# First activation tile on ScalarE's DMA queue, and FFN1's first pair of groups with P7 ahead of P5, in a float32 macaron block on one Trainium2 core

## Chip, core and metric

The kernel runs on one core of a Trainium2 chip. The metric is the device time of one execution in microseconds (us); the median of three timed executions of the kernel before is 2192.64 us (2191.59 to 2192.67).

TensorE (PE) does the matrix products and loads its weights beside them (PEld). VectorE (DVE) and ScalarE (ACT) prepare operands and take results out of the accumulator banks. SyncE (SP) issues transfers. GpSimd (POOL) does nothing here after its first microsecond.

## What is computed

A block over 1024 tokens of 1024 features, all in float32, cut to what matters:

```python
h = x + 0.5 * swiglu(rmsnorm(x), ffn1_w_in, ffn1_w_out)      # FFN1: D_FF = 2816
u = rmsnorm(h)
q, k, v, g_ret, p, gates = split(u @ w_in)
ret  = retention(rotary(q), rotary(k), v)  ...  * silu(g_ret)
pool = multiscale_pool(p)
h = h + (sigmoid(g0) * (ret @ w_ret_up) + sigmoid(g1) * (pool @ w_pool_up)) @ w_out
h = h + 0.5 * swiglu(rmsnorm(h), ffn2_w_in, ffn2_w_out)      # FFN2
out = rmsnorm(h)

def swiglu(x, w_in, w_out):
    gate, up = split(x @ w_in, 2)
    return (silu(gate) * up) @ w_out
```

The change touches only the first microseconds and the first three groups of FFN1's first product, `rmsnorm(x) @ ffn1_w_in`.

## The kernel before

**Layout.** Activations lie transposed: a tile has 128 features on the partitions and 1024 tokens along the row; `half(t, j)` is tokens 512j to 512j+511. `x` is eight such tiles, `x[0]` to `x[7]`, loaded in half tiles of 256 KB ("quarters"). A weight tile `raw` is 128 x 1024.

**Exact float32 products.** Every operand is split into a high and a low part: ScalarE rounds it into the high part (`split` line 146, or `split_scaled` line 150, which also multiplies by the norm's gain out of the tile `vec`), and VectorE subtracts (line 147 or 151) for the low part. `mm3` (lines 166 to 168) then issues three matmuls: high x high, high x low, low x high. Every matmul is preceded by a weight load. The names in the trace follow: `n1R` and `n1T` are FFN1's activation operands, `a_wL` and `a_wS` weight operands, digits left out.

**Strassen in seven products.** `strassen` (line 353) computes a 256-wide group of outputs, a gate tile and an up tile, from 2 x 2 blocks. The weight blocks are L11, L12 (the two halves of `ra`) and L21, L22 (of `rb`), with S1 = L21 + L22, S2 = S1 - L11, S3 = L11 - L21, S4 = L12 - S2. The activation blocks are R11, R12 (tiles 0 to 3, the two token halves) and R21, R22 (tiles 4 to 7), with T1 = R12 - R11, T2 = R22 - T1, T3 = R22 - R12, T4 = R21 - T2. The products use three accumulator banks:

- P1 = L11 R11 into bank a, which ScalarE copies into bank b (line 397)
- P2 = L12 R21 onto a; a is the result (0, 0), taken out by ScalarE (line 530)
- P6 = S2 T2 onto b; b is copied to v (line 402)
- P5 = S1 T1 onto b
- P7 = S3 T3 into bank e, copied to p7 by ScalarE (line 419)
- when both P5 and P7 are done, result (1, 1) = b + p7, by VectorE (`fourth` line 404, `evac` line 525). It reads b, so P3 of the same group can't write b before it is done
- P3 = S4 R22 onto b: result (0, 1), taken out by ScalarE (line 530)
- P4 = L22 T4 onto e: result (1, 0) = e + v, by VectorE (line 525)

A product has 4 x 3 = 12 matmuls of 128 x 128 by 128 x 512.

**The order of products.** `strassen` returns its steps at positions 0 to 6 in the order P1, P6, P5, P7, P2, P3, P4, each a pair (prepare the weights, do the product). `BY_OPERAND` = (0, 4, 1, 3, 2, 6, 5) is therefore P1, P2, P6, P7, P5, P4, P3. FFN1's groups come in the order 0, 11, 1, 12, 2, ... Group 0 is done without Strassen (`plain_group` line 579: 8 steps of 12 matmuls on R11, R21, R12, R22), so that TensorE can start while T1 to T4 are made. Groups 11 and 1 are the first pair: `in_turn` (line 449) takes each position for the one, then for the other. All later groups of FFN1 are done one at a time in the order P1, P7, P6, P2, P5, P4, P3.

**Program order.** `Flow.run` (line 64) issues the weight preparation of a step four steps ahead of its product, and after each product takes one piece of other work from a list (`flow.back`); a product that needs an operand takes pieces until it is there (`flow.until`). The list for FFN1 is filled at line 814: R11, R21, R12, gain on R22, R22, T2, T1, T3, T4, four pieces each (one for each pair of tiles), then eight pieces `x_square` (line 817: load a tile of x by tokens, square it on ScalarE and sum along the row), then `roots` (the norm's inverse roots, which use ScalarE's square root, line 201) and `rows` (spread over the partitions through TensorE, lines 219 and 335). The compiler's scheduler then arranges each engine's own sequence, with that order as its priority; on the chip each engine works through its sequence in order.

**Buffers that matter here.** Half tiles `c2`: 8, for the differences t1 (made with T2, read by T1), S1 to S4, v and p7. Weight operands `wt`: 5. Activation tiles `t4`: 9, of which x takes 8. Tiles `tl`: 4, of which group 0's results hold two and `x_square` uses the others.

**Loads at the start.** All transfers go through `load` (line 133), which is SyncE's queue: `vec` (line 176), then, from line 805, the weight block L11 of group 0, x[0] to x[3] tokens 0 to 511, L21, L12, x[4] to x[7], L22, then the second token half of x.

Of the kernel before, what the change touches and what calls it, by code (L numbers as in the profile page):

```python
# [20 lines left out]
KT = D // P  # L21
H = S // 2  # L22
# [30 lines left out]
BY_OPERAND = (0, 4, 1, 3, 2, 6, 5)  # L53
# [36 lines left out]
def block_kernel(ctx: ExitStack, tc, x, x_tok, vecs, f1_in, f1_out, w_in, pool_w, w_ret, w_pool, w_o,  # L90
                 f2_in, f2_out, rope, decay, consts, out):
    nc = tc.nc
# [21 lines left out]
    def raw(name):  # L114
        return sb.tile([P, S], F32, tag="raw", bufs=N_RAW, name=name)
# [4 lines left out]
    def t4(name):  # L120
        return sb.tile([P, S], F32, tag="t4", bufs=N_T4, name=name)

    def c2(name):
        return sb.tile([P, H], F32, tag="c2", bufs=N_C2, name=name)
# [8 lines left out]
    def load(dst, src):  # L133
        nc.sync.dma_start(dst, src)
# [4 lines left out]
    def half(t, j):  # L139
        return t[:, j * H : (j + 1) * H]  # L140
# [32 lines left out]
    vec = cp.tile([P, NV], F32, name="vec")  # L173
    neg = cp.tile([P, NV], F32, name="neg")
    cst = cp.tile([P, NC], F32, name="cst")
    load(vec, vecs)

    warm = cp.tile([P, 1], F32, name="warm")
# [68 lines left out]
    class Next(Norm):  # L247
# [22 lines left out]
        def g(self, mt, v=None):  # L270
            if self.gain is None:
                return None
            v = vec if v is None else v
            return v[:, self.gain + mt : self.gain + mt + 1]
# [174 lines left out]
    def in_turn(groups, order=range(7), first=2):  # L449

        groups = list(groups)
        steps = [g() for g in groups[:first]]
        for n in order:
            for g in steps:
                yield g[n]

        for g in groups[first:]:
            steps = g()
            for n in (0, 3, 1, 4, 2, 6, 5):
                yield steps[n]  # L460
# [49 lines left out]
    def ffn_in(nx, w, ops, name, start=None):  # L510

        R, T, B, T4 = ops
        hid = {}

        def group(g):
            gate_up = []

            def evac(which, in0, in1):
                if not gate_up:
                    new = tl if start and g == 0 else t4  # L520
                    gate_up.extend((new(f"{name}g{g}"), new(f"{name}u{g}")))
                tile, j = which
                dst = half(gate_up[tile], j)
                if in1 is not None:
                    tt(dst, in0, in1, ADD)
                elif nx.rb is not None:
                    tt(dst, in0, half(nx.rb, j), MUL)
                    return
                else:
                    copy(dst, in0)  # L530
                flow.add(lambda: tt(dst, dst, half(nx.rms(), j), MUL))

            def end():
                gate, up = gate_up

                def swish():
                    act(gate, gate, AF.Silu)

                def times(j):
                    tt(half(up, j), half(gate, j), half(up, j), MUL)  # L540

                flow.add(swish, lambda: times(0), lambda: times(1))
                hid[g] = up
                k = g % FH
                if g < FH:
                    return
                lo, hi, e = hid.pop(k), up, {}
                R11, R12, R21, R22 = half(lo, 0), half(lo, 1), half(hi, 0), half(hi, 1)

                def w1():  # L550
                    e["n"], e["m"] = t4(f"{name}n{k}"), c2(f"{name}m{k}")
                    tt(half(e["n"], 0), R12, R11, SUB)
                    tt(half(e["n"], 1), R22, R12, SUB)
                    load(B[k], e["n"])

                def w2():
                    tt(R12, R22, half(e["n"], 0), SUB)
                    load(R[k], lo)
                    load(T[k], hi)

                def w3():
                    tt(e["m"], R21, R12, SUB)
                    load(T4[k], e["m"])
                    done.add(k)

                flow.add(w1, w2, w3)

            if start and g == 0:
                return plain_group(nx, start, f"{name}{g}_", evac, end)
            return lambda: strassen(nx, w[g, 0], w[g, 1], f"{name}{g}_", evac, end)  # L570

        done = ops_done.setdefault(name, set())
        order = [g for k in range(FH) for g in (k, k + FH)]
        if start:
            return chain(group(0), in_turn((group(g) for g in order[1:]), (0, 4, 1, 2, 3, 5, 6)))
        return in_turn((group(g) for g in order), BY_OPERAND)


    def plain_group(nx, blocks, name, evac, end):

        t, w = {}, {}

        def step(o, i, j):


            def prep():
                if j == 0:
                    w[o, i] = weights(blocks[2 * o + i], f"{name}w{o}{i}")

            def body():  # L590
                if i == 0:
                    t[o] = bank(f"{name}{o}{j}")
                for k in range(4):
                    mm3(t[o], parts(w[o, i], k), parts(nx.operand(("R11", "R12", "R21", "R22")[2 * i + j], k)),
                        i == 0 and k == 0, i == 1 and k == 3)
                if i == 1:
                    evac((o, j), t[o], None)
                    if (o, j) == (1, 1):
                        end()

            return prep, body

        return [step(o, i, j) for j in range(2) for i in range(2) for o in range(2)]
# [189 lines left out]


    first = Next("n1", V_FFN1)
    xt = {mt: t4(f"x{mt}") for mt in range(KT)}
    ra, rb = raw("ra"), raw("rb")
    lead = half(ra, 0), half(ra, 1), half(rb, 0), half(rb, 1)

    def quarters(j, mts):  # L800
        for mt in mts:
            first.tiles[mt, j] = half(xt[mt], j)
            load(first.tiles[mt, j], x[mt, :, j * H : (j + 1) * H])

    load(lead[0], f1_in[0, 0, :, :H])
    quarters(0, range(4))
    load(lead[2], f1_in[0, 1, :, :H])
    load(lead[1], f1_in[0, 0, :, H:])
    quarters(0, range(4, 8))
    load(lead[3], f1_in[0, 1, :, H:])  # L810
    quarters(1, range(4))
    quarters(1, range(4, 8))
    load(cst, consts)
    first.work(first.r11, first.r21, first.r12, first.r22, first.p22, first.t2, first.t1, first.t3, first.t4_)
    x_sums = sb.tile([P, 8], F32, tag="ss", bufs=2, name="x_sums")

    def x_square(t):
# [14 lines left out]
    def ffn1():  # L832
        for n, step in enumerate(ffn_in(first, f1_in, ops1, "a", lead)):
            flow.rate = 1 if n < 40 else 2
            yield step
        yield from ffn_out(ops1, ops_done["a"], f1_out, x, "b", mix.quarter, end1)
# [133 lines left out]
    order = light[:2] + [o for two in zip(heavy, light[2:14]) for o in two] + light[14:]  # L970
# [401 lines left out]
    def second():  # L1372
        for n, step in enumerate(ffn_in(ffn2, f2_in, ops2, "c")):
            flow.rate = 1 if n < 14 else 2
            yield step
# [84 lines left out]
```

## Time and profile before

| | |
|---|---|
| timed, median of 3 | 2192.64 us (2191.59 to 2192.67) |
| the profiled execution's own time | 2192.35 us |
| its span, first to last instruction | 2190.6 us |
| TensorE's mean granted clock | 0.997 |
| first matmul on real data | 6.15 us |
| group 0 (96 matmuls) ends, P1 of group 11 begins | about 28.6 us |

The trace is of one execution. Times are microseconds from the first instruction. A row of the timeline gives start, duration, engine, line, operation, what it writes and reads, its size, how many were merged, and in brackets how long the engine was idle before it and what ended that. Matmuls are pipelined, so a matmul row's duration is longer than the distance to the next; distances between starts are used below for TensorE's pace.

### The profile page before, as it was taken

What the parts mean: (1) busy time and instruction counts of PE and PEld (TensorE: products, weight loads), DVE (VectorE), ACT (ScalarE), POOL (GpSimd) and SP (SyncE); (2) the same over time, 40 slices, a digit from 0 to 9 for tenths busy, and PEclk for the clock granted to TensorE, in tenths of its full rate; (3) what the DMA queues carried; (4) which work ended last, traced back from release to release, by engine and by line L of the source; (5) the groups of instructions that cost most, each with busy time, mean ns of one, the idle gap of its engine ahead of it and who ended that gap; (6) DMA issues with size and microseconds to landing.
All of it is one profiled execution on the core that took longest, in us unless ns stands there. A gap on an engine that the chain in (4) does not pass through costs nothing.

```text
span 2190.6 us, 27454 instructions
## 1 busy us (share of the span) xinstructions
PE 2171.6 (99%) x10070; PEld 1809.5 (83%) x10070; DVE 1677.5 (77%) x2766; ACT 985.3 (45%) x1756; POOL 0.2 (0%) x4
## 2 busy tenths in 40 slices
PE   9999999999999999999999999999999999999998
PEld 7788888888888888888888998878888888888887
DVE  8687777887786767677776777799977777689775
ACT  8433333444553433434336664446533333344451
POOL 0000000000000000000000000000000000000000
PEclk9999999999999999999999999999999999999999
DMA  6144222495323333323235557524242323249522
GB/s 239 58 154 168 92 104 96 162 334 178 125 92 112 139 116 116 115 105 127 96 124 187 188 180 278 192 87 147 75 144 101 135 92 123 94 158 337 173 73 78
DMA packets 111015, 311.86 MB, mean 142 GB/s; under 512 B 12448, under 2 KB 14624, under 8 KB 110880
## 3 DMA queue, kind: packets, MB, share of 16 engines
q1 hardware_dynamic: 110880, 310.11, 40.0%
q8 instruction: 79, 1.29, 0.2%
q14 instruction: 56, 0.46, 0.1%
HBM read 219.36 MB, written 90.70 MB: 142 GB/s over the span
## 4 chain that ended last, share of the span: by engine, by line
PE 94%; DVE 3%; ACT 2%; DMA 1%; issue 0%; SPq 0%; DVEq 0%; ACTq 0%
PE c_b L166 3%; PE c_b L168 3%; PE c_b L167 3%; PE a_b L168 2%; PE a_b L166 2%; PE a_b L167 2%; PE c_e L166 2%; PE c_a L167 2%; PE c_a L166 2%; PE c_a L168 2%; PE c_e L168 2%; PE c_e L167 2%; PE a_e L168 2%; PE a_e L167 2%; PE a_a L168 2%; PE a_e L166 2%
## 5 line engine op out<-in xcount | busy, mean ns | idle before, releaser
L146 ACT CAST c_wS<-c_S 128x512 fp32r<-128x512 f32 x88 | 54.7, 622 | 124.7 <-PE c_b L168 76.1
L146 ACT CAST a_wS<-a_S 128x512 fp32r<-128x512 f32 x84 | 52.2, 622 | 105.7 <-PE a_b L168 71.0
L147 DVE TENSOR_TENSOR c_wS<-c_S,c_wS 128x512 fp32r<-128x512 f32 x88 | 60.9, 692 | 22.6 <-ACT c_wS L146 22.0
L147 DVE TENSOR_TENSOR a_wS<-a_S,a_wS 128x512 fp32r<-128x512 f32 x84 | 58.2, 693 | 24.4 <-ACT a_wS L146 24.0
L167 PE MATMUL c_a<-n3R,c_wL 128*128 128x512 f32 x176 | 68.6, 390 | 0.0
L167 PE MATMUL c_b<-n3T,c_wS 128*128 128x512 f32 x176 | 68.5, 389 | 0.0
L168 PE MATMUL c_b<-n3T,c_wS 128*128 128x512 f32 x176 | 68.5, 389 | 0.0
L168 PE MATMUL c_a<-n3R,c_wL 128*128 128x512 f32 x176 | 68.5, 389 | 0.0
L166 PE MATMUL c_a<-n3R,c_wL 128*128 128x512 f32 x176 | 68.3, 389 | 0.0
L166 PE MATMUL c_b<-n3T,c_wS 128*128 128x512 f32 x176 | 68.2, 389 | 0.0
L168 PE MATMUL a_a<-n1R,a_wL 128*128 128x512 f32 x168 | 65.4, 389 | 0.0
L166 PE MATMUL a_a<-n1R,a_wL 128*128 128x512 f32 x168 | 65.4, 389 | 0.0
L167 PE MATMUL a_a<-n1R,a_wL 128*128 128x512 f32 x168 | 65.4, 389 | 0.0
L166 PE MATMUL a_b<-n1T,a_wS 128*128 128x512 f32 x168 | 65.4, 389 | 0.0
L167 PE MATMUL a_b<-n1T,a_wS 128*128 128x512 f32 x168 | 65.4, 389 | 0.0
L168 PE MATMUL a_b<-n1T,a_wS 128*128 128x512 f32 x168 | 65.4, 389 | 0.0
L146 ACT CAST c_wL<-c_ra 128x512 fp32r<-128x512 f32 x44 | 27.2, 620 | 38.0 <-PE c_e L168 38.0
L146 ACT CAST a_wL<-a_ra 128x512 fp32r<-128x512 f32 x42 | 26.0, 621 | 37.6 <-PE a_e L168 37.6
L167 PEld LDWEIGHTS c_a<-n3R,c_wL 128*128 128x128 f32 x176 | 33.0, 188 | 7.2 <-DVE n3R L151 0.3
L167 PEld LDWEIGHTS c_b<-n3T,c_wS 128*128 128x128 f32 x176 | 33.0, 188 | 7.0 <-DVE n3T L151 0.2
L147 DVE TENSOR_TENSOR c_wL<-c_ra,c_wL 128x512 fp32r<-128x512 f32 x44 | 30.4, 692 | 10.8 <-ACT c_wL L146 10.5
L168 PEld LDWEIGHTS c_a<-n3R,c_wL 128*128 128x128 f32 x176 | 33.0, 188 | 6.9
(2500 smaller groups left out, 7300.3 us busy)
## 6 DMA issues: line engine op xcount, KB each, us to landing
c_ra<-in_f_in SPq DMA_DIRECT2D x22, 512.0 KB, 3.7
c_rb<-in_f_in SPq DMA_DIRECT2D x22, 512.0 KB, 4.7
a_ra<-in_f_in SPq DMA_DIRECT2D x21, 512.0 KB, 4.5
a_rb<-in_f_in SPq DMA_DIRECT2D x21, 512.0 KB, 5.1
t<-au SPq DMA_DIRECT2D x11, 512.0 KB, 2.6
b<-an SPq DMA_DIRECT2D x11, 512.0 KB, 3.2
r<-au SPq DMA_DIRECT2D x11, 512.0 KB, 3.8
br<-r SPq DMA_DIRECT2D x11, 512.0 KB, 5.4
```

The costliest lines, as they stand in the source:

```text
L146: copy(hi, src)
L147: tt(lo, src, hi.bitcast(F32), SUB)
L166: mm(dst, w[0], m[0], start=start, stop=False, skip_group_check=True)
L167: mm(dst, w[0], m[1], start=False, stop=False, skip_group_check=True)
L168: mm(dst, w[1], m[0], start=False, stop=stop, skip_group_check=True)
```

## The change

Two things are edited. `x[0]`'s first token half is loaded by a transfer that ScalarE issues, at the top of the program, before `vec`; right behind it SyncE issues the load of L11 of group 0, and only then `vec`. (For this the tiles `xt`, `ra` and `rb` are allocated earlier.) And the first pair of groups uses `BY_OPERAND`: P1, P2, P6, P7, P5, P4, P3 in place of P1, P2, P6, P5, P7, P3, P4; in the list of other work T3 comes before T1.

```diff
@@ block_kernel, before the loads
+    xt = {mt: t4(f"x{mt}") for mt in range(KT)}
+    ra, rb = raw("ra"), raw("rb")
+    nc.scalar.dma_start(half(xt[0], 0), x[0, :, :H])
+    load(half(ra, 0), f1_in[0, 0, :, :H])
     load(vec, vecs)
@@ ffn_in
         if start:
-            return chain(group(0), in_turn((group(g) for g in order[1:]), (0, 4, 1, 2, 3, 5, 6)))
+            return chain(group(0), in_turn((group(g) for g in order[1:]), BY_OPERAND))
@@ the loads of FFN1
     first = Next("n1", V_FFN1)
-    xt = {mt: t4(f"x{mt}") for mt in range(KT)}
-    ra, rb = raw("ra"), raw("rb")
     lead = half(ra, 0), half(ra, 1), half(rb, 0), half(rb, 1)
 
     def quarters(j, mts):
         for mt in mts:
             first.tiles[mt, j] = half(xt[mt], j)
-            load(first.tiles[mt, j], x[mt, :, j * H : (j + 1) * H])
-
-    load(lead[0], f1_in[0, 0, :, :H])
+            if (mt, j) != (0, 0):
+                load(first.tiles[mt, j], x[mt, :, j * H : (j + 1) * H])
+
     quarters(0, range(4))
...
-    first.work(first.r11, first.r21, first.r12, first.r22, first.p22, first.t2, first.t1, first.t3, first.t4_)
+    first.work(first.r11, first.r21, first.r12, first.r22, first.p22, first.t2, first.t3, first.t1, first.t4_)
```

## Prediction

> **What bounds the kernel now.** I read the page first.
>
> ```profile
> span 2190.6 us, 27454 instructions
> PE 2171.6 (99%) x10070; PEld 1809.5 (83%) x10070; DVE 1677.5 (77%) x2766; ACT 985.3 (45%) x1756; POOL 0.2 (0%) x4
> ```
>
> TensorE is busy 99% of the span, and the change removes no matmul, so it can win only what TensorE stands idle or runs slowly. Next I read who TensorE waits for over the whole span (total, times, longest, in us):
>
> ```profile
> PE a_b L166 <- DVE au L525: 2.2, 1, 2.2
> ...
> PE wo1b L166 <- ACT wo1wS L146: 1.6, 1, 1.6
> ...
> PE a L166 <- ACT n1R L150: 0.8, 1, 0.8
> ...
> PE wo1b L168 <- DVE wo1wS L147: 0.4, 1, 0.4
> ```
>
> The list is short, and its longest entry lies where the order of products is changed; the one for `a` is the first matmul on real data, where the load is changed. The timeline of TensorE round the longest:
>
> ```profile
> 55.82 0.39 PE L166 MATMUL a_b<-n1R,a_wS 128*128 128x512 f32 x1
> ...
> 58.31 0.39 PE L168 MATMUL a_b<-n1R,a_wS 128*128 128x512 f32 x1
> 60.88 0.50 PE L166 MATMUL a_b<-n1R,a_wS 128*128 128x512 f32 x1 [2.18 <-DVE au L525]
> ...
> 65.23 0.48 PE L166 MATMUL a_e<-n1T,a_wL 128*128 128x512 f32 x1
> ```
>
> The first row begins P3 of group 11, the second is its twelfth matmul: 11 steps in 2.49 us, a pace of 0.226 us. P3 of group 1 begins at 60.88 and should have begun at 58.31 + 0.23 = 58.54: 2.34 us lost. Its own 12 matmuls then take 65.23 - 60.88 = 4.35 us where 12 x 0.226 = 2.72 are due: 1.63 us more. The windows (length, busy us of each engine, granted clock, DMA) show why:
>
> ```profile
> 58.58:62.00 3.42, 1.24 (x6) 0.95 (x6) 2.55 (x6) 2.82 (x6) 0.00 (x0) 1.00 0.10 38
> 62.00:65.41 3.41, 3.41 (x10) 2.67 (x9) 1.77 (x7) 0.00 (x0) 0.00 (x0) 0.50 0.00 0
> 1474.97:1478.40 3.43, 1.80 (x7) 0.92 (x6) 3.43 (x7) 1.88 (x4) 0.00 (x0) 1.00 0.21 77
> ```
>
> Behind a stretch of 3.42 us in which TensorE was busy for 1.24, the granted clock is 0.50 for 3.41 us. The third row is the other large stall, before `wo1b`: busy 1.80 in a stretch as long, and the clock stays. The stall of this pair thus costs 2.34 + 1.63 = 3.97 us.
>
> **Where this stall comes from.** ScalarE, then VectorE, before it:
>
> ```profile
> 52.99 0.62 ACT L146 CAST n1T<-x 128x512 fp32r<-128x512 f32 x1
> ...
> 56.74 1.06 ACT L820 ACTIVATE xs<-xs 128x1024 f32<-128x1024 f32 x1 [2.13 <-DMA xs<-in_x_tok]
> ...
> 57.91 1.28 ACT L201 ACT_TABLE_LOAD   x1
> 59.21 0.21 ACT L201 ACTIVATE n1r<-n1v 128x8 f32<-128x8 f32 x1
> 59.32 0.57 ACT L419 COPY a_p<-a_e 128x512 f32<-128x512 f32 x1
> ...
> 60.14 0.68 DVE L525 TENSOR_TENSOR au<-a_b,a_p 128x512 f32<-128x512 f32 x1
> ```
>
> P7 of group 1 is done when P3 of group 11 begins, at 55.82. Its bank is copied (line 419) only at 59.32, because ScalarE, which works in order, stands before the eighth square of x (its tile lands at 56.74), then loads a table and does the norm's root. Only after that copy can VectorE form b + p7, and only then may P3 write b. TensorE stands behind P3.
>
> **The change part by part.** *P7 before P5, P4 before P3.* Counting 24 matmuls back from 55.82 twice, the pair's fourth position begins at 50.38 and its third at 44.94. So far 44.94 was P5, 50.38 P7, 55.82 P3, 61.3 P4 (had nothing stalled). Now P7 runs from 44.94, P5 from 50.38, P4 from 55.82, P3 from 61.3. P7 of group 1 ends 5.4 us earlier, at 50.4; its copy is needed by its P4 at 58.5 and its sum by P3 at 64.0. Were that copy to stay as late as now, sum ready at 60.82, P3 would still not wait. The 3.97 us go. No instruction is added or taken away; it costs nothing if the operands keep up with the new due times, and their cover is this:
>
> ```profile
> 45.00:50.50 5.50, 5.50 (x26) 4.57 (x25) 5.50 (x10) 4.91 (x10) 0.00 (x0) 1.00 0.71 239
> 43.79 1.31 DVE L147 TENSOR_TENSOR n1T<-x,n1T 128x512 fp32r<-128x512 f32 x2
> ...
> 45.65 0.70 DVE L147 TENSOR_TENSOR a_wS<-a_S,a_wS 128x512 fp32r<-128x512 f32 x1
> ...
> 53.73 0.69 DVE L147 TENSOR_TENSOR n1T<-x,n1T 128x512 fp32r<-128x512 f32 x1
> ```
>
> VectorE (third busy column) works without a pause until 50.5, so lateness is the danger. T3's last low part is the first of the two merged at 43.79, ready near 44.5; P7's fourth operand is due 9 matmuls after 44.94, at 47.0. The weights S3 of group 1 (by their place in VectorE's sequence the row at 45.65) are ready at 46.35 and due at 47.66 + 0.45 = 48.1. T4's last part, at 53.73, is ready at 54.42 and due at 55.82 + 2.04 = 57.9. All three would be in time even if made no earlier than now, and the change moves T3 ahead. Two costs are not in the trace: the eight `c2` tiles, which t1 holds longer when T1 comes after T3, and the scheduler's new sequence on each engine. Bounds for both together: 0 (all due times kept) to a wait as long as the one removed, 2.34 us. I take 0, since the margins above are 1.7 to 3.5 us.
>
> Following the list of other work by hand, the squares, the roots and `rows` come two products earlier than before. Their three stalls on ScalarE remain; then nothing due soon stands behind the eighth: S4's weights for group 1, due at 64.0, are the next. One evacuation, P3 of group 12, finds the norm's rows there and goes to VectorE as one multiplication in place of a copy and a later multiplication; its 0.7 us (as the row at 60.14) take the place of the same 0.7 us later, so I cost it at nothing.
>
> *x[0] on ScalarE's queue.* The chain at the start:
>
> ```profile
> 1.17 0.42 SPq L134 DMA_DIRECT2D ra<-in_f_in  x1
> 1.21 4.11 PE L188 MATMUL set<-zero 128*128 128x512 bf16 x12 [1.21 <-DVE zero L183]
> 1.64 3.65 DMA x<-in_x
> 3.86 0.62 ACT L146 CAST a_w<-ra 128x512 fp32r<-128x512 f32 x1 [1.64 <-DMA ra<-in_f_in]
> 5.37 0.73 ACT n1R L150
> 6.13 0.76 DVE n1R L151
> 6.94 0.50 PE a L167
> ```
>
> x[0] is issued third, lands at 1.64 + 3.65 = 5.29, is rounded from 5.37 and subtracted from 6.13; TensorE's second matmul follows at 6.94, and from there it never waits until the stall above. L11 lands near 3.86. The change issues x[0] and L11 side by side, both without `vec` in front: SyncE's first transfer starts one issue (1.64 - 1.17 = 0.47 us) earlier. `vec`, needed by the same rounding, is now behind L11. Lower bound: both land together at 5.29 - 0.47 = 4.82, ScalarE does the weight's cast first (0.62 us) and rounds x[0] near 5.4 as now: gain 0, and below it -0.3 if `vec` is late. Upper bound: x[0] takes the 2.7 us that L11 took from its issue (1.17 to 3.86), landing near 3.4 with L11, cast until 4.0, rounding at once: 1.4 us, of which TensorE's warming matmuls, which end at 5.32 (the row at 1.21), leave about 1.3 before 6.94. Between: 512 KB in flight from the start should land near 4.35, cast until 4.97, rounding at once. I take 0.4. ScalarE's own work at the start is a table load (1.28 us in the row at 57.91) and one square of a single column; with an issue of 0.42 us ahead of them it is done near 2.7, before anything lands that it could work on, so the issue is hidden.
>
> [...]
>
> *Sum*, against the profiled execution's 2192.35 us (span 2190.6): 2192.35 - 3.97 - 0.4 = 2187.98, say **2188.0 us**. The median of the runs shown, 2192.64, is 0.29 above that execution, so the same sum on it would give 2188.3; I stay with the traced one.
>
> **Rivals.**
>
> *A. The half clock comes back at another stall.* From the rows, 1.24 us busy in 3.42 loses the clock and 1.80 does not. All later work arrives 4.4 us earlier, and the 3.41 us stretches need not move with it. The two waits of `wo1b` (1.6 and 0.4 us) are not both in the stretch of the third row; where one stretch holds them both, TensorE's 1.80 us there shrink by about 0.4 towards 1.24, and if the next is halved it is +1.63: 2189.6. Against: it takes the right phase. [...]
>
> *B. A new wait in the pair.* T3 needs two VectorE operations where T1 needs one, on an engine without a pause, and S3's sum needs a `c2` tile that t1 may hold. If S3 or T4 slips by its margin and 1.5 to 2 us more, TensorE waits that long, too short for the clock: 2188.0 + 1.8 = 2189.8. For it: the full VectorE column; against: the margins.
>
> *C. P4 falls behind the eighth square.* If the scheduler puts T4's last rounding or L22's cast (T4's is now at 52.99) after the square and the root on ScalarE, its high part is ready at 59.3 + 0.6 = 59.9 in place of 55.4, where P4 now begins: 4.5 us of wait plus 1.63 of half clock, 2188.0 + 6.1 = 2194.1, slower than before. It decides when P4's due time, now 5.5 us earlier, falls behind that square's end at 57.8; should the pair's second half wait again it passes 2197. Against: L22's buffers come free two products earlier too.
>
> *D. The load does nothing*, 2188.4, or all it can, 2187.1: these are the forecast's own ends.
>
> **How the numbers follow.** Forecast (stall gone, own range 2187.0 to 2189.0) 0.60, A 0.13, B 0.15, C 0.12. The range 2186.8 to 2192.2 holds the first three nearly whole, 0.85, and cuts off C. A measurement of this kernel tells about 0.2% from no change: 4.39 us of 2192.64, so "faster" means under 2188.25. The forecast lies just below that line: 0.44 of its 0.60 there, the rest above. Within 0.2%: 0.16 + 0.13 + 0.15 + 0.05 of C = 0.49; I give 0.03 of it to A and B with a better start, hence faster 0.47, same 0.46, slower 0.07.
>
> **What would show it.** Right: no wait of `a_b` for line 525; no half clock near 62; the matmuls of P4 of group 1 follow those of group 11 at 0.226 us; the second matmul near 6.5. Wrong: a TensorE wait between 44 and 62 for `n1T`, `a_wS` or `a_wL`, a clock of 0.50 elsewhere, or a second matmul still at 6.9.

## The result, and the profile after

The changed kernel takes **2189.05 us** (median of 22 executions, 2188.01 to 2190.84) where the kernel before, run beside it, takes 2191.72 us (22 executions, 2189.78 to 2194.93). The ratio is 0.9987, 95% interval 0.9981 to 0.9993: 2.7 us, 0.12%. The forecast was 2188.0; the measured time lies in its range and on the "within 0.2%" side of the line.

The profiled execution of the changed kernel took 2188.59 us, against 2192.35 us of the one profiled before. The head of its page, the same two lines as before:

```profile
span 2186.7 us, 27454 instructions
PE 2171.2 (99%) x10070; PEld 1808.2 (83%) x10070; DVE 1677.8 (77%) x2766; ACT 984.9 (45%) x1755; POOL 0.2 (0%) x4
```

The span is 3.9 us shorter and TensorE's busy time the same within 0.4 us, but not all of the gain is idle time: a stretch at half clock counts as busy (3.41 of 3.41 us in the prediction's window from 62.00). What busy time was saved there came back in part at the start, where the warming matmuls took 5.13 us in this execution and 4.11 in the one before:

```profile
1.21 5.13 PE L193 MATMUL set<-zero 128*128 128x512 bf16 x12 [1.21 <-DVE zero L188]
```

Who TensorE waits for (total, times, longest):

```profile
PE wo1b L166 <- ACT wo1wS L146: 1.6, 1, 1.6
...
PE wo1b L168 <- DVE wo1wS L147: 0.4, 1, 0.4
...
PE a_b L166 <- DVE au L530: 0.3, 1, 0.3
```

The 2.2 us of `a_b`, first of the list before, are gone (the operation is line 530 now, since the edit moves lines down); the 0.3 us that is left belongs to another place, shown below. The pair itself, TensorE's timeline: the first rows of P1 of group 11, P4 of groups 11 and 1, P3 of groups 11 and 1, and P1 of group 12.

```profile
28.90 0.39 PE L166 MATMUL a_a<-n1R,a_wL 128*128 128x512 f32 x1
...
56.10 0.39 PE L166 MATMUL a_e<-n1T,a_wL 128*128 128x512 f32 x1
...
58.82 0.39 PE L166 MATMUL a_e<-n1T,a_wL 128*128 128x512 f32 x1
...
61.54 0.39 PE L166 MATMUL a_b<-n1R,a_wS 128*128 128x512 f32 x1
...
64.26 0.39 PE L166 MATMUL a_b<-n1R,a_wS 128*128 128x512 f32 x1
...
66.98 0.39 PE L166 MATMUL a_a<-n1R,a_wL 128*128 128x512 f32 x1
```

The last four distances are 2.72 us each, 12 matmuls at 0.227. From P1 of group 11 to P1 of group 12 lie 14 products, 14 x 2.72 = 38.08 us, and the rows give 66.98 - 28.90 = 38.08: the pair loses nothing. In the trace before, the same two rows are

```profile
28.62 0.39 PE L166 MATMUL a_a<-n1R,a_wL 128*128 128x512 f32 x1
...
70.82 0.39 PE L166 MATMUL a_a<-n1R,a_wL 128*128 128x512 f32 x1
```

42.20 us apart, a loss of 4.12. This distance is used for every kernel below. Windows of the changed kernel (length, busy us of each engine, clock, DMA), first the stretches of the pair, then the two that share the stall before `wo1b`:

```profile
58.58:62.00 3.42, 3.42 (x17) 2.82 (x16) 1.65 (x4) 2.41 (x4) 0.00 (x0) 1.00 0.01 4
62.00:65.41 3.41, 3.41 (x17) 2.83 (x16) 1.98 (x7) 2.21 (x5) 0.00 (x0) 1.00 0.00 0
1470.37:1473.78 3.41, 2.39 (x10) 1.42 (x8) 3.41 (x7) 1.02 (x3) 0.00 (x0) 1.00 0.22 82
1473.78:1477.19 3.41, 2.38 (x9) 1.71 (x10) 3.41 (x6) 2.66 (x5) 0.00 (x0) 1.00 0.00 0
```

In the first two TensorE is busy throughout, and the clock stays at 1.00 in all four. Why the pair no longer stalls, on ScalarE's timeline:

```profile
48.14 0.59 ACT L424 COPY a_p<-a_e 128x512 f32<-128x512 f32 x1 [0.30 <-PE a_e L168]
...
51.24 0.57 ACT L424 COPY a_p<-a_e 128x512 f32<-128x512 f32 x1
...
59.58 1.06 ACT L823 ACTIVATE xs<-xs 128x1024 f32<-128x1024 f32 x1 [2.65 <-DMA xs<-in_x_tok]
...
60.63 0.60 ACT L146 CAST a_wS<-a_S 128x512 fp32r<-128x512 f32 x1
61.25 1.28 ACT L206 ACT_TABLE_LOAD   x1
62.55 0.21 ACT L206 ACTIVATE n1r<-n1v 128x8 f32<-128x8 f32 x1
```

Both copies of P7 are done by 51.8, long before the eighth square. That square still waits for its tile (2.65 us) and starts even later than before, at 59.58 against 56.74, with table load and root behind it; but the copies no longer stand there, and TensorE, which has P3 of group 1 to begin at 64.26, does not wait for any of it.

In this execution the start went the other way. The chain of work of the changed kernel's first microseconds (start, length, what):

```profile
0.73 4.34 DMA ra<-in_f_in
...
5.09 0.38 ACT a_w L146
...
5.62 0.73 ACT n1R L150
...
6.37 0.76 DVE n1R L151
...
7.18 0.50 PE a L167
```

The load of x[0] that ScalarE issues (at 0.73), its size and its time to landing:

```profile
x<-in_x ACTq DMA_DIRECT2D x1, 256.0 KB, 4.5
```

Before, x[0] was the last to land, at 5.29, and L11 had landed at about 3.86, 2.7 us after its issue. Now L11 takes 4.34 us from its issue and lands at 5.07, and x[0] lands near 5.2, hardly earlier than before. The rounding of x[0], which stands behind the weight's cast on ScalarE, begins at 5.62 where it began at 5.37; the second matmul comes at 7.18, not at 6.94 or at the forecast's 6.5.

**Where the 3.6 us between the two traces lie.** The last matmul begins at 2183.25 before and at 2179.66 after. P1 of group 11 begins 0.28 later, the pair is 4.12 shorter, and 0.59 is given back before the first matmul of the next stage, nearly all of it at P3 of FFN1's last group:

```profile
428.22 0.50 PE L166 MATMUL a_b<-n1R,a_wS 128*128 128x512 f32 x1 [0.27 <-DVE au L530]
```

This small wait (0.54 us in distances between starts) is in some executions of several kernels, the old order among them, and in others of the same kind not. The rest is won: 0.66 us at `xb` (a product with `state`, at 1196 us in the trace before), whose wait for ScalarE is 0.40 us in place of 1.06, less about 0.3 us given back in small pieces behind it.

### The profile page after: what moved, and what is told of

The parts are those of the page before. It is cut to its first block, busy times and chain, and to the rows that moved or that the text cites. A ratio compares the mean times of both kernels' runs of the same rounds, so it can differ in the third digit from the quotient of the medians.

```text
span 2186.7 us, 27454 instructions
## 1 busy us (share of the span) xinstructions
PE 2171.2 (99%) x10070; PEld 1808.2 (83%) x10070; DVE 1677.8 (77%) x2766; ACT 984.9 (45%) x1755; POOL 0.2 (0%) x4
## 4 chain that ended last, share of the span: by engine, by line
PE 94%; DVE 3%; DMA 1%; ACT 1%; issue 0%; DVEq 0%; ACTq 0%; SPq 0%
PE c_b L166 3%; PE c_b L167 3%; PE c_b L168 3%; PE a_b L166 3%; PE a_b L168 3%; PE a_b L167 3%; PE c_e L166 2%; PE c_a L167 2%; PE c_e L167 2%; PE c_a L166 2%; PE c_a L168 2%; PE c_e L168 2%; PE a_e L168 2%; PE a_a L168 2%; PE a_e L167 2%; PE a_a L167 2%
## 5 line engine op out<-in xcount | busy, mean ns | idle before, releaser
L167 PEld LDWEIGHTS c_a<-n3R,c_wL 128*128 128x128 f32 x176 | 33.0, 188 | 7.1 <-DVE n3R L151 0.3
L147 DVE TENSOR_TENSOR a_wL<-a_ra,a_wL 128x512 fp32r<-128x512 f32 x42 | 28.9, 691 | 12.9 <-ACT a_wL L146 12.6
```

The lines of the kernel that those rows point to most:

```text
L147: tt(lo, src, hi.bitcast(F32), SUB)
L167: mm(dst, w[0], m[1], start=False, stop=False, skip_group_check=True)
```

## The experiments

Each profile is one execution. In the table, "P1 of 11" is where P1 of group 11 begins, "pair" the distance from there to P1 of group 12 (38.08 is no loss), both from the traces; the ratio is to the kernel before, timed beside it. Each kernel ran 11 times and the kernel before 33 times beside it (22 and 22 for the changed kernel); e1 to e4, e5 to e8 and e9 to e12 are three sets, each timed on a chip of its own. The last column is the mean difference with a 95% interval from the scatter of the executions. It is narrower than the ratio's interval, and by the ratio's only the changed kernel (both rows), e4 and e10 stand clear of no change.

| kernel | P1 of 11 | pair | ratio (95%) | us against before |
|---|---|---|---|---|
| before (the profile above) | 28.62 | 42.20 | | |
| changed (the profile above) | 28.90 | 38.08 | 0.9987 (0.9981 to 0.9993) | -2.7 ± 0.6 |
| e3_before_again | 29.56 | 39.64 | 1.0 (0.9991 to 1.0009) | -0.2 ± 0.6 |
| e1_order_only | 29.76 | 38.08 | 0.9994 (0.9985 to 1.0003) | -1.2 ± 0.5 |
| e12_order_again | 29.20 | 38.08 | 0.9991 (0.9982 to 1.0) | -1.9 ± 0.6 |
| e2_load_only | 28.83 | 39.55 | 0.9995 (0.9986 to 1.0004) | -1.1 ± 0.6 |
| e6_change_again | 29.17 | 38.08 | 0.9989 (0.998 to 0.9998) | -2.4 ± 0.7 |
| e5_no_eighth_load | 29.21 | 39.57 | 0.9993 (0.9984 to 1.0001) | -1.2 ± 0.8 |
| e10_no_root_no_eighth | 29.58 | 39.20 | 0.9989 (0.998 to 0.9998) | -2.1 ± 0.8 |
| e11_no_root | 29.29 | 39.93 | 0.9993 (0.9984 to 1.0002) | -1.5 ± 0.9 |
| e4_order_vec_act | 28.87 | 38.08 | 0.999 (0.9981 to 0.9999) | -2.1 ± 0.5 |
| e7_order_vec_third | 29.39 | 38.08 | 0.9994 (0.9985 to 1.0003) | -1.5 ± 0.7 |
| e8_change_vec_first | 29.13 | 38.08 | 0.9992 (0.9983 to 1.0001) | -1.6 ± 0.7 |
| e9_change_vec_act | 29.93 | 38.08 | 0.9993 (0.9984 to 1.0002) | -1.4 ± 0.6 |

### The two parts alone, and the kernel before once more

e1_order_only and e12_order_again make the edits of the order alone:

```diff
-            return chain(group(0), in_turn((group(g) for g in order[1:]), (0, 4, 1, 2, 3, 5, 6)))
+            return chain(group(0), in_turn((group(g) for g in order[1:]), BY_OPERAND))
...
-    first.work(first.r11, first.r21, first.r12, first.r22, first.p22, first.t2, first.t1, first.t3, first.t4_)
+    first.work(first.r11, first.r21, first.r12, first.r22, first.p22, first.t2, first.t3, first.t1, first.t4_)
```

> The order of the pair alone, all loads on SyncE as before. Theory 1 (the whole gain is the pair's stall; the load costs a little): no wait of a_b for line 525, TensorE's second matmul at 6.9 as before, P1 of group 12 begins near 66.7 (0.3 earlier than in the changed kernel), and the time is the changed kernel's less about 0.3 us: 2188.5 to 2189.0 beside a median of 2191.7 before. Rival (the load is worth something that the start of the trace doesn't show, for instance in the second loads): P1 of group 12 not before 67.0, time not below the changed kernel's 2189.05.

> The new order alone, old loads, once more, beside the others on this chip. Theory M: P1 of group 11 begins at 29.4 or later with a wait of ScalarE for x[2], P1 of group 12 follows 38.1 later, and the time is 1.0 to 1.6 us below the kernel before, about 1 us behind the changed kernel with vec on ScalarE. Rival (the load gives nothing, and the 1 us between the two before was chance): P1 of group 11 at 28.7 or earlier, and a time 2.2 us or more below.

e2_load_only makes the edits of the load alone:

```diff
+    nc.scalar.dma_start(half(xt[0], 0), x[0, :, :H])
+    load(half(ra, 0), f1_in[0, 0, :, :H])
     load(vec, vecs)
...
-            load(first.tiles[mt, j], x[mt, :, j * H : (j + 1) * H])
-
-    load(lead[0], f1_in[0, 0, :, :H])
+            if (mt, j) != (0, 0):
+                load(first.tiles[mt, j], x[mt, :, j * H : (j + 1) * H])
+
```

> The first load on ScalarE's queue alone, the pair's order as before. Theory 1: L11 and x[0] both land near 5.1, the second matmul comes near 7.2 in place of 6.9, the pair's wait for line 525 stays at 2 to 2.3 us (it ends with the eighth square, whose transfer doesn't depend on the start), and the time is that of before, within 0.5 us (0.3 lost at the start is partly taken out of the stall). Rival (x[0] early is a gain of 0.4 as forecast): second matmul near 6.5 and 0.4 us less.

e3_before_again is the kernel before, with no edit.

> The kernel before once more, with the granted clock of each of its runs and a second profile. Theory 2 (a stretch of half clock depends on where the 3.41 us stretches lie against the stall, not on the stall alone): the stall of 2.2 us is there again, but the clock's boundaries lie elsewhere, the loss behind it may be anything from 0 to 1.7 us, and the runs of one program spread over 2 us or more. Rival (the stall always loses the clock): half clock behind it again, 1.6 us, and runs within 1 us but for outliers.

What came of these expectations: e1's P1 of group 12 begins at 67.84 and its time is not below the changed kernel's, so its rival holds, and theory 1, in which the load costs a little, falls. e12 lies between its two accounts, with 29.20 and -1.9 us. In e2 the second matmul comes at 7.01, but TensorE waits 1.2 us in the pair, not 2 to 2.3, and the time is 1.1 us less, so neither of its accounts holds. e3 lost no clock, as theory 2 allowed, behind a shorter stall than it assumed.

The new order gives a pair of 38.08 us in every one of the eight traces that have it; the old order, wherever nothing is left out, 39.55, 39.64 and, in the profile of before, 42.20. The repeat of the kernel before shows the difference. Its ScalarE round the stall, and TensorE's P3 of group 1:

```profile
56.78 1.06 ACT L820 ACTIVATE xs<-xs 128x1024 f32<-128x1024 f32 x1 [1.43 <-DMA xs<-in_x_tok]
...
57.95 1.28 ACT L201 ACT_TABLE_LOAD   x1
...
59.36 0.57 ACT L419 COPY a_p<-a_e 128x512 f32<-128x512 f32 x1
```

```profile
60.91 0.50 PE L166 MATMUL a_b<-n1R,a_wS 128*128 128x512 f32 x1 [1.26 <-DVE au L525]
```

The eighth square, the copy behind it and P3 stand within 0.04 us of where they stood in the profile of before (56.74, 59.32, 60.88): the stall's end is set by the landing of the eighth tile. But this execution began P1 of group 11 0.94 us later (29.56), so P3 was due later, at 29.56 + 11 x 2.72 = 59.48, and waited 1.43 us in place of 2.34; and no half clock follows (the clock is 1.00 from 62.89 to 66.30). With the old order a late start is thus swallowed by the stall; with the new one it shows in full. So what the order is worth in the traces is 1.5 to 1.6 us, and 4.1 where the start is early and the clock is lost. The timed runs, -1.2 ± 0.5 and -1.9 ± 0.6, agree with the smaller figure. The load alone is worth -1.1 ± 0.6, and the parts (about -1.6 as a mean of the two, and -1.1) add up to the -2.4 and -2.7 of the whole. In the old order an earlier start as such should be lost in the stall. In e2's trace it isn't, because the eighth square also starts earlier:

```profile
55.95 1.06 ACT L823 ACTIVATE xs<-xs 128x1024 f32<-128x1024 f32 x1 [1.33 <-DMA xs<-in_x_tok]
```

P3 of group 1 follows 4.13 us later, at 60.08, and P1 of group 12 comes at 68.38, 0.82 us ahead of the repeat of before (69.20). Whether the changed loads bring the eighth tile earlier or this is chance, one trace can't tell: in the three traces of the old order with the old loads and the eighth tile, that square begins at 56.74, 56.78 and 57.67.

### What makes the stall: the tile, or what ScalarE does behind it

e5_no_eighth_load leaves the eighth token tile's transfer out, in the old order; the eighth square reads the seventh tile again:

```diff
+    last = {}
...
-        r = tl(f"xs{t}")
-        load(r, x_tok[t])
+        if t < 7:
+            last["r"] = tl(f"xs{t}")
+            load(last["r"], x_tok[t])
+        r = last["r"]
```

> The kernel before, but the eighth square reads the seventh tile again, whose load is the last; the eighth tile is not loaded. Theory 1 (the pair's wait ends with the landing of the eighth tile, which holds up ScalarE's copy of P7): ScalarE's squares end by 53, the copy for group 1 follows its P7 at once (near 56.3), TensorE doesn't wait for line 525 with the old order of products, P1 of group 12 begins about 38.1 us after P1 of group 11, and the time is that of the order alone (1.4 us below before). Rival (old order itself is too tight, P3 waits for VectorE's sum anyway): a wait of 1 us or more at the same place and at most 0.5 us less.

The pair took 39.57 us: the stall stayed, which was a miss. ScalarE, then TensorE, of that kernel:

```profile
54.51 1.06 ACT L824 ACTIVATE xs<-xs 128x1024 f32<-128x1024 f32 x1
...
55.56 0.56 ACT L419 COPY a_p<-a_e 128x512 f32<-128x512 f32 x1
...
56.66 1.28 ACT L201 ACT_TABLE_LOAD   x1
...
58.08 0.57 ACT L419 COPY a_p<-a_e 128x512 f32<-128x512 f32 x1
```

```profile
56.91 0.50 PE L166 MATMUL a_b<-n1R,a_wS 128*128 128x512 f32 x1 [0.33 <-DVE au L525]
...
60.48 0.50 PE L166 MATMUL a_b<-n1R,a_wS 128*128 128x512 f32 x1 [0.55 <-DVE au L525]
```

and VectorE, from the norm's inverse to the sum b + p7 of group 1:

```profile
58.20 0.20 DVE L202 RECIPROCAL n1r<-n1r 128x8 f32<-128x8 f32 x1 [0.75 <-ACT n1r L201]
...
59.74 0.68 DVE L525 TENSOR_TENSOR au<-a_b,a_p 128x512 f32<-128x512 f32 x1
```

With no tile to wait for, the square moves up to 54.51, ahead of group 11's copy too. That copy makes P3 of group 11 wait a little, and table load and root still stand ahead of group 1's, so the same stall comes back as two shorter ones. Nor is the copy the last link: it ends at 58.65, and the sum begins 1.09 us later, because VectorE first waits for the root and then does the rest of the norm's small operations and a sum for S. So the root holds the stall up on two engines. The tile's landing was one cause among three (with the square itself, and the table load and root); two more kernels take out the root (VectorE multiplies by 1 in its place), alone and with the transfer:

```diff
-        act(r0, v, AF.Sqrt)
+        act(r0, v, AF.Sqrt) if name != "n1" else nc.vector.tensor_scalar(r0, v, 1.0, None, ALU.mult)
```

> The kernel before, in its old order, without the load of the eighth token tile (its square reads the seventh tile again) and with the first norm's square root left out (a multiplication by 1 on VectorE stands in its place, so ScalarE loads no table there and does no root). Theory K (the stall is the sum of what stands ahead of the copies of P7 on ScalarE: late tile, square, table load and root): the copy of group 1 moves from 58.1, where it stood without the load alone, to 56.7; no wait before P3 of group 1; what stays is the wait before P3 of group 11, about 0.5 us, behind the eighth square. From P1 of group 11 to P1 of group 12: 38.5 to 38.7 us, against 39.57 without the load alone and 38.08 in the new order. Rival L (the old order itself costs, since b is read by VectorE and then written at once by P3): 39.0 or more.

> The kernel before, old order, eighth tile loaded as before, with only the first norm's square root left out as above. Theory K: the eighth square still starts when its tile lands (55.9 to 56.8), and group 1's copy follows it at once, at 57.1 to 57.9 in place of 58.5 to 59.3; P3 of group 1 begins at 58.6 to 59.4, 0.1 to 0.9 us late, and P1 of group 12 comes 38.2 to 39.0 us after P1 of group 11. No half clock behind it, since 0.9 us idle is far under the 2.29 us of the window that lost it. Rival (the late tile alone makes the stall): 39.5 or more, as in the kernel before.

e10_no_root_no_eighth, ScalarE, then its one wait of TensorE for line 525:

```profile
55.12 1.06 ACT L824 ACTIVATE xs<-xs 128x1024 f32<-128x1024 f32 x1
...
56.17 0.57 ACT L419 COPY a_p<-a_e 128x512 f32<-128x512 f32 x1
...
57.15 0.58 ACT L419 COPY a_p<-a_e 128x512 f32<-128x512 f32 x1
```

```profile
57.77 0.50 PE L166 MATMUL a_b<-n1R,a_wS 128*128 128x512 f32 x1 [0.83 <-DVE au L525]
```

The wait before P3 of group 1 is gone, as theory K had it. The one before P3 of group 11 is longer than it expected, since the square began at 55.12 and not at 54.51: P3 was due at 29.58 + 10 x 2.72 = 56.78 and began 0.99 late. From 57.77 to P1 of group 12, at 68.78, are 11.01 us for four products, 10.88: the old order as such costs no more than 0.13 us, so rival L falls, though the 39.20 us of the pair are in its span.

e11_no_root, ScalarE, then TensorE:

```profile
57.67 1.06 ACT L820 ACTIVATE xs<-xs 128x1024 f32<-128x1024 f32 x1 [2.03 <-DMA xs<-in_x_tok]
...
58.72 0.57 ACT L419 COPY a_p<-a_e 128x512 f32<-128x512 f32 x1
```

```profile
60.93 0.50 PE L166 MATMUL a_b<-n1R,a_wS 128*128 128x512 f32 x1 [1.56 <-DVE au L525]
```

The pair's 39.93 us are a miss and lie in the rival's span: the eighth square could start only at 57.67, when its tile had landed, a microsecond later than assumed. The distances within the chain do not depend on that. From the start of the eighth square to P3 of group 1 are 60.88 - 56.74 = 4.14 us in the profile of before, 60.91 - 56.78 = 4.13 in its repeat, and 60.93 - 57.67 = 3.26 here: the root and its table load are worth 0.87 us of the stall (the copy comes 1.5 us sooner behind the square, but VectorE does the norm's small operations and a sum for S first, and begins b + p7 only at 60.19, 0.9 us behind the copy's end). The stall is thus: landing of the tile, plus 4.13 us, less the time at which P3 is due. The new order takes the pair out of the whole chain at once, since both the copies on ScalarE and the sum on VectorE (at 57.40) stand ahead of it.

### What the load is worth, and through what

The changed kernel once more, and three other ways to share the head of the queues. e4_order_vec_act and e7_order_vec_third keep x[0] on SyncE behind L11 and put `vec` on ScalarE's queue, or third on SyncE; e8_change_vec_first is the change with `vec` ahead of L11, as before; e9_change_vec_act is the change with `vec` on ScalarE behind x[0].

```diff
 e4_order_vec_act, against the kernel before (with the new order)
-    load(vec, vecs)
+    nc.scalar.dma_start(vec, vecs)
```

```diff
 e7_order_vec_third, against the changed kernel
-    nc.scalar.dma_start(half(xt[0], 0), x[0, :, :H])
     load(half(ra, 0), f1_in[0, 0, :, :H])
+    load(half(xt[0], 0), x[0, :, :H])
     load(vec, vecs)
```

```diff
 e8_change_vec_first, against the changed kernel
-    load(half(ra, 0), f1_in[0, 0, :, :H])
     load(vec, vecs)
+    load(half(ra, 0), f1_in[0, 0, :, :H])
```

```diff
 e9_change_vec_act, against the changed kernel
-    load(vec, vecs)
+    nc.scalar.dma_start(vec, vecs)
```

> The pair's new order, and in place of x[0] the 32 KB of vec go over ScalarE's queue, so that SyncE issues L11 first and x[0] second, one issue (0.44 us) earlier than before. Theory 1 (the order in which L11 and x[0] land decides; side by side they land together): L11 lands near 3.4, x[0] near 4.85, the second matmul comes near 6.5 (no earlier than 0.2 us behind the warming matmuls, which end between 5.3 and 6.4 by the clock), and the time is 0.4 us below the run with the order alone. Rival (two queues at once are slow whatever they carry): x[0] not before 5.3 and the second matmul at 6.9 or later.

> The changed kernel once more, for its times beside the next two and a second profile. Theory 3 (x[0] on a second queue keeps group 0 from starving): group 0 runs without a wait behind its second matmul, P1 of group 11 begins by 28.9 again, median 2189.0 to 2189.3. Rival (the starving at 8 to 9 us in the two profiles with all loads on SyncE was chance): P1 of group 11 may begin near 29.7 here as well.

> New order, all loads on SyncE, but vec third, behind L11 and x[0]. Theory 3 (the second queue is what helps): as the order alone, P1 of group 11 as often near 29.6 as near 28.6, median 2190.0 or more. Rival, theory 4 (vec, 128 rows of 256 bytes at the head of the queue, is what delays the large loads behind it): P1 of group 11 near 28.4 (x[0] one issue earlier, 0.4 us), median 2189.0 or less.

> The changed kernel with vec ahead of L11 on SyncE's queue, x[0] still on ScalarE's. Theory 3: as the changed kernel, 2189.0 to 2189.4, P1 of group 11 by 29.0 (L11 a little later, vec earlier). Theory 4: the loads behind vec starve group 0 as in the kernel with the order alone, P1 of group 11 near 29.6 in the profile if it is frequent, median 2190.0 or more.

> The changed kernel, with vec issued by ScalarE behind x[0], so that SyncE's queue starts with L11 and x[1]. Theory M (group 0 starves for x[2] when SyncE carries everything at the head; ScalarE's queue takes load off it): x[2] is rounded without a wait of ScalarE, P1 of group 11 begins at 28.6 to 28.9, P1 of group 12 follows 38.1 later, and the time stands 2.1 to 3.0 us below the kernel before. Rival N (vec behind x[0] is now the last of the three to land, and the gain product needs it): the second real matmul at 7.4 or later, P1 of group 11 at 29.2 or later, and the time 1 to 2 us below.

With the old loads group 0 often waits a second time, for x[2]. e1_order_only, ScalarE's rounding of x[2] and x[3], and the wait of TensorE that follows:

```profile
7.90 1.38 ACT L150 ACTIVATE n1R<-x,vec 128x512 fp32r<-128x512 f32 x2 [1.18 <-DMA x<-in_x]
```

```profile
8.67 0.50 PE L166 MATMUL a<-n1R,a_w 128*128 128x512 f32 x1 [0.33 <-ACT n1R L150]
```

x[2] came 1.18 us after ScalarE was ready for it. In the repeat of before the same wait is 1.01 us and P1 of group 11 begins at 29.56; in the profile of before it isn't there (28.62). With the changed loads the roundings follow each other without a break in the changed kernel's first trace, and the wait is 0.33 us in its second. P1 of group 11 begins at 29.32 as a mean of the seven traces with the old loads (28.62 to 29.76) and at 28.97 in the three with the changed ones (28.83 to 29.17): 0.35 us, with overlapping spans. The timed gain is larger, 1.1 ± 0.6 alone and, as -2.4 and -2.7 less -1.2 and -1.9, about 1.0 on top of the order. Whether the part above 0.35 us is there at all, and where, stays open.

Nor do the variants settle it. With `vec` ahead again (e8) the gain on top of the order is gone, and e7 without the second queue has none either, as if both were needed; but e4, which leaves x[0] on SyncE, is at -2.1 ± 0.5, and these differ by less than their intervals. The trace of e8 points to what keeps x[0] late in the changed kernel. ScalarE's first rounding there:

```profile
4.21 0.72 ACT L150 ACTIVATE n1R<-x,vec 128x512 fp32r<-128x512 f32 x1 [1.55 <-DMA x<-in_x]
```

With L11's 256 KB one issue later, x[0] on the same second queue is rounded 1.4 us earlier than in the changed kernel's profile, and the second matmul comes at 6.74; x[2] is then 0.86 us late, and group 11 begins at 29.13 all the same.

Of the other expectations, e4's second matmul (6.62) and start of group 11 (28.87) speak for its theory 1 and against its rival, though its cast of L11 begins at 4.35 and not near 3.4. The medians of e7 and e8, 2189.62 and 2189.60, lie between the spans of their theories. e6 began group 11 at 29.17, later than theory 3 had it. e9 is clear in its trace, in favour of rival N. ScalarE, then TensorE:

```profile
6.69 2.57 ACT L150 ACTIVATE n1R<-x,vec 128x512 fp32r<-128x512 f32 x4 [0.67 <-DMA vec<-in_vecs]
```

```profile
7.46 0.50 PE L166 MATMUL a<-n1R,a_w 128*128 128x512 f32 x1 [0.97 <-ACT n1R L150]
```

`vec` lands last, and the first matmul comes 1.07 us later than in the changed kernel (6.39). None of the four variants is faster than the changed kernel.

### The half clock elsewhere

The traces of e2_load_only, e6_change_again and e12_order_again lose the clock behind the stall before `wo1b`. Windows of e6_change_again, then of e8_change_vec_first, which does not:

```profile
1470.75:1474.16 3.41, 1.78 (x8) 1.12 (x7) 3.41 (x6) 1.66 (x3) 0.00 (x0) 1.00 0.22 82
1474.16:1477.58 3.42, 3.17 (x8) 2.15 (x7) 3.42 (x7) 2.41 (x5) 0.00 (x0) 0.50 0.00 0
```

```profile
1471.10:1474.52 3.42, 1.79 (x8) 1.03 (x7) 3.42 (x7) 1.75 (x4) 0.00 (x0) 1.00 0.22 81
1474.52:1477.93 3.41, 2.98 (x14) 2.18 (x12) 3.41 (x7) 2.42 (x6) 0.00 (x0) 1.00 0.00 0
```

In all these kernels the stall itself is the same: by the distances between starts, 1.80 and 0.59 us are lost before `wo1b`. What differs, by the author's estimate, is where stretches of 3.41 us cut it. The estimate is made from the clock of two traces. In the profile of before it becomes 1.00 at 3.97 us, 0.50 at 62.00, 1.00 at 65.41 and 0.50 at 2181.68; in the changed kernel's it becomes 1.00 at 6.05 and 0.50 at 2180.34. The distances, 58.03, 3.41, 2116.27 and 2174.29 us, are 17, 1, 620 and 637 times 2174.29 / 637 = 3.4133. Counted on in such steps, the stretch at this stall in the profile of before is not the prediction's third row but 1475.12:1478.53, with TensorE busy 1.78; it kept the clock too (1.00 from 1478.53 to 1481.95). In e2_load_only TensorE was busy 1.36 in 1473.15:1476.56, so that one stretch held both waits, and the clock was 0.50 from 1476.56 to 1479.97. In the changed kernel's first profile a cut falls, by the same count, in the middle of the stall, at 1473.78, busy 2.39 on one side and 2.38 on the other (the windows shown with the result), and the clock stayed. The price, from the first matmul of `wo0a` (the product with w_out) to the first of `c_a` (FFN2): 79.25 to 79.29 us in the eleven traces without (79.25 in the profile of before, 1462.23 to 1541.48), 80.13 to 80.58 in the three with; TensorE's busy time over the span is 2170.0 to 2171.6 us in the eleven and 2172.2 to 2172.4 in the three.

## Why the prediction was right, and where it was not

**The stall goes: right, step by step.** No wait of `a_b` for line 525 (now 530) in the pair, no half clock near 62, P4 of group 1 behind P4 of group 11 at 0.227 us per matmul. The due times held: the sum b + p7 of group 1 runs from 57.40 to 58.08 on VectorE, 6.2 us before P3 of group 1 begins, and nothing waits for T3, S3 or T4. The three pieces on ScalarE that the forecast left standing are there (square at 59.58, table load, root), and behind the eighth nothing was due. Two readings were off without harm: the eighth square came 2.84 us later than before (59.58 against 56.74), not two products earlier, and the stall had been followed through ScalarE alone, where VectorE too stood behind the norm's operations (e5, e11). Rivals B and C did not come.

**The 3.97 us: right for the traced execution, too large for the kernel.** The step that failed is the base: the sum is made "against the profiled execution's 2192.35 us", with "I stay with the traced one". That execution lost 4.12 us in the pair, 0.15 more than the forecast took out; but it began group 11 earlier than any of the other six traces with the old loads, and none of the other five in the old order lost the clock behind this stall. The repeat of the kernel before lost 1.56 us, and the timed worth of the order is 1.2 to 1.9 us. The other side of the same choice is that the kernel before takes 2191.72 us as a median over 22 executions, not 2192.35. The mis-sized term is thus 1.63 us of half clock, taken as certain, and the idle time, 2.34 taken and 1.43 in the repeat.

**x[0] on ScalarE's queue, 0.4 us: the mechanism failed at its place.** The forecast put the gain at the second matmul, at 6.5; it came at 7.18, 7.03 and 7.01 in the three traces of these loads, against 6.79 to 7.57 in the seven of the old loads (6.94 and 6.88 in the two of the kernel before). The means are 7.07 and 7.06: nothing was gained there. "Between: 512 KB in flight from the start should land near 4.35" is the step: L11 landed at 5.07 and x[0] near 5.2, so the forecast's lower bound holds, both landing together, and even later than its 4.82. With x[0] issued at the same moment L11 took 4.34 us, in place of the 2.7 (1.17 to 3.86) that it took with x[0] issued 0.47 us behind it. The forecast had the two land 0.5 us behind L11's 3.86; L11 came 1.2 us behind it and x[0] 1.4. What the load gives comes later, at x[2], which the forecast did not look at: 0.35 us in the traces at P1 of group 11, about 1.0 in the timed runs, so the size of this term stays open between 0.4 and 1.6 us.

**The sum.** -4.37 us was forecast against the traced execution, -2.7 measured: the order was put 2.1 to 2.7 us too high, the load up to 1.2 too low. The two errors partly cancel, and the nearness of 2188.0 to 2189.05 owes something to that.

**Rival A: real, but not tied to this change.** The half clock behind `wo1b` came in one trace of the load alone, one of the order alone and one of the changed kernel, at 0.9 to 1.3 us and not the 1.63 that the forecast gave it. Of the two executions of the changed kernel one lost the clock there and the other kept it: in e6_change_again TensorE was busy 1.78 of the 3.41 us before half clock set in, at 1474.16, so the wait of 1.6 us lies whole in that stretch; in the first profile, which shows no half clock there, the wait ends at 1474.39, and the estimated cut at 1473.78 falls into it (2.39 and 2.38). That the place of the cut decides is not shown: e8_change_vec_first, with 1.79, kept the clock.

## What to carry to other kernels

A stall whose end is set by a transfer and whose start moves with the work before it differed here from one execution to the next (2.34 us in one trace of the kernel before, 1.43 in the other), so its worth is read from two or three profiles, and a half clock behind it, which the first of the two had and the second not, is a chance to be weighed and not a fixed term. Where several pieces of side work stand ahead of a copy that is due, taking out one of them can move the others up (without the eighth tile's load the pair still took 39.57 us); putting the copy, and the sum that reads it, ahead of them all needs no instruction and took the whole stall (38.08). The second issuing queue did not by itself bring the first transfer earlier (x[0] landed near 5.2 us in place of 5.29); look at what else is issued at the same moment, and at which tile the engines starve for next.

## What the runs showed of the hardware

- Stretches of 3.41 us in which TensorE was busy 1.24 (before, 58.58:62.00), 1.36 (e2, 1473.15:1476.56), 1.78 (e6, 1470.75:1474.16) and 1.79 us (e12, 1470.49:1473.90) were followed by as long a stretch at a clock of 0.50. Others with 1.78 (before, 1475.12:1478.53), 1.79 (e8, 1471.10:1474.52) and 1.84 (the changed kernel, 2173.51:2176.93) were followed by 1.00. What decides at 1.78 and 1.79 the traces can't tell.
- Executions of one kernel differ by up to 5 us (2189.78 to 2194.93 for the kernel before), and their traces in where group 11 begins, by 0.94 us between the two of the kernel before, where one of them waited 1.01 us for a single 256 KB tile.
- With x[0] issued by ScalarE at the same moment, L11 (256 KB) took 4.34 us from issue to landing, where it took 2.7 with x[0] issued 0.47 us behind it. Its cast on ScalarE begins at 4.93 to 5.09 us in the three traces of the first kind and at 3.83 to 4.24 in the seven of the second, though it is issued 0.44 us earlier in the first.
